# A decoder block with a product-key expert layer: the first gather tile's second half turned into a fifth dense tile

## The chip, the cores and the metric

One core of one Trainium2 chip. The metric is the device time of one execution in microseconds (us); a time of the kernel is the median of several runs. A profile is one execution more, with its own time. The engines are TensorE (PE; its weight loads are PEld), VectorE (DVE), ScalarE (ACT), GpSimd (POOL) and SyncE (SP). Each runs its instructions in the order in which they are written, and waits for the others through semaphores. SP and GpSimd issue the DMA transfers here.

## The reference

1024 tokens of width 1024 pass a mixing layer (two causal convolutions between an input and an output projection, with norms) and then the expert layer, which is nearly all of the time:

```python
q = (xf @ w_q).reshape(n_tok, PEER_HEADS, PEER_D_KEY)         # 8 heads
s1 = jnp.einsum("thd,hnd->thn", q[..., :128], sub_keys[:, 0])  # 128 keys
s2 = jnp.einsum("thd,hnd->thn", q[..., 128:], sub_keys[:, 1])
v1, i1 = lax.top_k(s1, 16)
v2, i2 = lax.top_k(s2, 16)
vals, pos = lax.top_k((v1[..., :, None] + v2[..., None, :]).reshape(..., 256), 16)
idx = e1 * 128 + e2            # e1, e2: i1, i2 at pos; 16384 experts
gates = jax.nn.softmax(vals, axis=-1)
u_sel = jnp.take(u, idx, axis=0)       # u, v: 16384 x 1024 float32, 64 MB each
act = jax.nn.gelu(jnp.einsum("chkd,cd->chk", u_sel, xc))
v_sel = jnp.take(v, idx, axis=0)
out = jnp.einsum("chk,chkd->cd", act * gates, v_sel)
```

So each token takes 8 x 16 = 128 rows of u and 128 rows of v, weighted by a gelu and a gate. The result is added to the token's row and normalised.

## The kernel before

The 1024 tokens are 8 tiles of 128. Tiles 0 to 3 (`NG`) are gather tiles: their rows of u and v are fetched one per token by indirect DMA (`fetch`, 128 x 1024 floats, 512 KB a step), 128 steps of u and 128 of v for each tile. In a u step VectorE multiplies the rows with the token's row and sums (L719); after the 128th the weights `w` are gelu times gate. In a v step VectorE adds w times the rows to the sum `prow` (L756). For tile 0 every second v step is done by ScalarE (scale, L761) and GpSimd (add to `h2`, L762).

Tiles 4 to 7 (`ND` = 4) are dense tiles: all 16384 experts are computed for their 512 tokens, and the gates decide. u and v are walked in 128 chunks of 128 experts, chunk c being all experts with first key c. For a chunk, `prep_u` transposes the rows of u on TensorE in two halves, ScalarE casts the high half `uhi`, a product with minus the identity (`minus`, L864) subtracts it, and ScalarE casts what is left as `ulo`. `hidden` multiplies in three passes (high by high, high by low, low by high: `mm3`, lines 213 to 215), 12 products of 128 x 512 for each half of the chunk. Then p = gelu, times the gates (GpSimd, L947), split into `phi` (ScalarE) and `plo` (GpSimd). Rows of v are split into `vhi` (ScalarE, L181) and `vlo` (GpSimd, L182), four buffers of each. After each group of four chunks (`GRP`), `down` multiplies the four p with the four v for all dense tiles: 8 outputs of 12 products, each added to `acc` by VectorE (L917). The rows of u and v share three buffers, `raw`.

Stages, in order: the front (projections, convolutions, norms) for tokens 0 to 511; keys, the queries of the gather half and the routing of tile 0; the front for tokens 512 to 1023 (`front(1)`), in which the gather steps begin; the routing of the dense tiles (`queries`); the gate stage (`gate_matrix`); the dense stage (`dense`). In the gate stage the experts and gates of a dense tile become one-hot rows, 8 tokens at a time (o2 and o1; of the 8 tokens of o1, `X` are done by ScalarE from a narrow one-hot `ob`, the others by VectorE, L823), and one product per token (L828) makes its 128 x 128 matrix of gates, which SP writes to memory (`gd`, L841), 32 tokens at a time, in runs of `QUAD` key chunks x 32 tokens x 4 bytes. Beside it `hidden_ahead` already computes p before the gates for the chunks in `AHEAD` (24) and stores them (`pd`, by one buffer `pa`); the dense stage loads those and computes the other 104.

The gather steps are a generator (`steps`) that the other code pulls: `advance(n)` adds n to a debt and takes a step for each whole one. The constants `PROJ`, `OUT`, `QUERY`, `GATE`, `AHD`, `HIDE`, `PACE` are what each piece of other work pulls: so they set how many gathers are issued in each stage. A gather's use comes five steps (`LAG`) behind its issue; nine buffers hold the rows. While a tile gathers, the routing of the next is done in small steps (`route_later`, every `EVERY`-th step). The order on each engine is settled when the program is built, by priorities; `mark` and `after` tie a gather's use behind the last marked instruction of its engine.

## Time and profile before

| | |
|---|---|
| median of 3 runs | 3099.85 us (3089.3 to 3113.24) |
| the profiled execution | 3104.55 us, span on the core 3102.8 us |
| TensorE, matmuls busy | 2499.2 us (81%) |
| VectorE busy | 2222.1 us (72%) |
| GpSimd busy | 1974.8 us (64%) |
| ScalarE busy | 1138.9 us (37%) |
| DMA | 838.28 MB, mean 270 GB/s |
| mean granted clock of TensorE | 0.904 |

Busy time is the share in which an engine has an instruction in hand; register, branch and semaphore instructions don't count. Matmuls overlap, and a matmul's duration includes the time in which the next has begun; the distance from start to start is what one costs in a row. "A <- B" in a wait means that the instruction A stood still until B had ended. [...] DMA share is the mean busy share of the core's 16 DMA engines.

### The profile page before, as it was taken

The page shows a single profiled execution, that of the slowest core. Times are in us where ns is not written, and L with a number is a line of the kernel's source. Part 1 is how long each engine was busy: PE and PEld are TensorE (multiplying, and loading weights), DVE is VectorE, ACT ScalarE, POOL GpSimd, SP SyncE. Part 2 cuts the span into 40 slices and gives each one's busy share as a digit, 9 for nine tenths or more (in the row PEclk, how much of TensorE's full clock was granted, in tenths as well). Part 3 has the DMA queues.
Part 4 walks back from the last instruction along what each step waited for, and adds up shares of the span by engine and source line. Part 5 has one row for each costly group of instructions (what it writes and reads, how often), then busy time and mean ns, then how long its engine had stood idle before and what let it go on. Part 6 is the DMA issues. An engine that isn't in the chain of part 4 may idle for free.

```text
span 3102.8 us, 36426 instructions
## 1 busy us (share of the span) xinstructions
PE 2499.2 (81%) x12256; PEld 2035.8 (66%) x12256; DVE 2222.1 (72%) x4518; ACT 1138.9 (37%) x1951; POOL 1974.8 (64%) x1569
## 2 busy tenths in 40 slices
PE   7988887135774688987989989899999898988993
PEld 6877675135553567775767767677777776767772
DVE  6975499899999988894565756565657565657566
ACT  3234322215433786773323233323232333232321
POOL 0002377948988533345878777778777778787774
PEclk9988999566887799998999999999999999999997
DMA  3234389776766578998989888898888888988886
GB/s 105 79 105 159 103 283 344 211 292 218 219 205 229 184 241 285 319 326 299 334 308 331 321 294 317 300 335 319 329 314 322 307 322 316 326 323 325 310 303 245
DMA packets 366571, 838.28 MB, mean 270 GB/s; under 512 B 25849, under 2 KB 184569, under 8 KB 362288
## 3 DMA queue, kind: packets, MB, share of 16 engines
q0 software_dynamic: 147456, 536.94, 48.4%
q1 hardware_dynamic: 218304, 296.85, 28.5%
q8 instruction: 96, 1.57, 0.2%
q10 hardware_dynamic: 624, 2.18, 0.2%
q14 instruction: 91, 0.75, 0.1%
HBM read 782.38 MB, written 53.48 MB: 269 GB/s over the span
## 4 chain that ended last, share of the span: by engine, by line
PE 25%; POOL 14%; issue 11%; DVE 5%; ACT 4%; DMA 4%; SPq 1%; POOLq 0%; another core or an unknown queue 0%; DVEq 0%; ACTq 0%
PE ms L215 7%; POOL g L694 7%; PE ms L214 7%; PE ms L213 7%; POOL vlo L182 4%; POOL p L947 2%; PE mm L828 2%; DVE g L719 2%; DMA raw<-in_peer_v_dram 1%; DVE prow L756 1%; PE tr L864 1%; PE tr L858 1%; ACT o L821 1%; POOL plo L182 1%; DMA g<-in_peer_u_dram,ix 1%
## 5 line engine op out<-in xcount | busy, mean ns | idle before, releaser
L694 POOL DMA_INDIRECT g<-in_peer_u_dram,ix x512 | 504.4, 985 | 389.7 <-DVE g L719 158.2
L719 DVE SCALAR_TENSOR_TENSOR g<-g,prow 128x1024 f32<-128x1024 f32 x512 | 607.5, 1216 | 119.4 <-DMA g<-in_peer_u_dram,ix 117.1
L694 POOL DMA_INDIRECT g<-in_peer_v_dram,ix x512 | 500.1, 977 | 235.1 <-DVE prow L756 120.8
L756 DVE SCALAR_TENSOR_TENSOR prow<-g,w,prow 128x1024 f32<-128x1024 f32 x450 | 578.3, 1285 | 52.7 <-DMA g<-in_peer_v_dram,ix 44.6
L917 DVE TENSOR_TENSOR acc<-acc,ms 128x512 f32<-128x512 f32 x256 | 175.6, 686 | 472.9 <-PE ms L215 409.3
L215 PE MATMUL ms<-nhi,ulo 128*128 128x512 f32 x1024 | 430.8, 421 | 33.0 <-ACT ulo L865 31.4
L213 PE MATMUL ms<-nhi,uhi 128*128 128x512 f32 x1024 | 441.6, 431 | 3.1 <-ACT pa L887 3.1
L214 PE MATMUL ms<-nlo,uhi 128*128 128x512 f32 x1024 | 424.4, 414 | 0.0
L213 PE MATMUL ms<-vhi,phi 128*128 128x512 f32 x1024 | 402.1, 393 | 1.2 <-ACT phi L181 1.2
L215 PE MATMUL ms<-vhi,plo 128*128 128x512 f32 x1024 | 399.3, 390 | 1.2 <-POOL plo L182 1.2
L214 PE MATMUL ms<-vlo,phi 128*128 128x512 f32 x1024 | 399.2, 390 | 0.0
L182 POOL TENSOR_TENSOR wlo<-wraw,whi 128x1024 fp32r<-128x1024 f32 x60 | 144.0, 2400 | 356.6 <-ACT whi L181 355.6
L182 POOL TENSOR_TENSOR vlo<-raw,vhi 128x1024 fp32r<-128x1024 f32 x128 | 307.1, 2404 | 40.1 <-ACT vhi L181 38.9
L181 ACT CAST vhi<-raw 128x1024 fp32r<-128x1024 f32 x128 | 131.2, 1049 | 505.0 <-PE ms L215 352.4
L215 PEld LDWEIGHTS ms<-nhi,ulo 128*128 128x128 f32 x1024 | 203.3, 199 | 91.4 <-ACT ulo L865 42.8
L864 PE MATMUL tr<-uhi,minus 128*128 128x512 f32 x256 | 123.7, 485 | 139.8 <-ACT uhi L862 132.8
L213 PEld LDWEIGHTS ms<-nhi,uhi 128*128 128x128 f32 x1024 | 205.4, 201 | 37.7 <-ACT pa L887 3.4
L214 PEld LDWEIGHTS ms<-nlo,uhi 128*128 128x128 f32 x1024 | 205.2, 200 | 33.1
L215 PEld LDWEIGHTS ms<-vhi,plo 128*128 128x128 f32 x1024 | 192.4, 188 | 42.5 <-POOL plo L182 2.0
L213 PEld LDWEIGHTS ms<-vhi,phi 128*128 128x128 f32 x1024 | 192.7, 188 | 40.9 <-ACT phi L181 1.6
L214 PEld LDWEIGHTS ms<-vlo,phi 128*128 128x128 f32 x1024 | 192.8, 188 | 38.1
L862 ACT CAST uhi<-tr 128x512 fp32r<-128x512 f32 x256 | 149.3, 586 | 143.4 <-PE tr L858 121.1
(213 smaller groups left out, 5110.3 us busy)
## 6 DMA issues: line engine op xcount, KB each, us to landing
raw<-in_peer_u_dram SPq DMA_DIRECT2D x128, 512.0 KB
raw<-in_peer_v_dram SPq DMA_DIRECT2D x128, 512.0 KB
gd<-st SPq DMA_DIRECT2D x64, 512.0 KB
g<-gd SPq DMA_DIRECT2D x32, 1024.0 KB
wraw<-in_w_in_dram SPq DMA_DIRECT2D x40, 512.0 KB
wraw<-in_peer_w_q_dram SPq DMA_DIRECT2D x32, 512.0 KB
wraw<-in_w_out_dram SPq DMA_DIRECT2D x16, 512.0 KB
g<-in_peer_u_dram,ix POOLq DMA_INDIRECT x512
```

The costliest lines, as they stand in the source:

```text
L181: nc.scalar.copy(hi, src)
L182: self.mark(eng.tensor_tensor(lo, src, hi.bitcast(F32), op=OP.subtract))
L213: self.nc.tensor.matmul(ps, lh(a), rh(b), start=first and i == 0, stop=False)
L214: self.nc.tensor.matmul(ps, lh(a), rl(b), start=False, stop=False)
L215: last = self.nc.tensor.matmul(ps, ll(a), rh(b), start=False, stop=final and i == n - 1)
L694: self.nc.gpsimd.indirect_dma_start(out=g, out_offset=None, in_=self.t[table][0], in_offset=bass.IndirectOffsetOnAxis(ap=ix, axis=0))
L719: self.after(nc.vector.scalar_tensor_tensor(ut, ut, 1.0, b["x"], op0=OP.mult, op1=OP.mult, accum_out=b["act"][:, k:k + 1]))
L756: self.after(nc.vector.scalar_tensor_tensor(b["h"], g, w, b["h"], op0=OP.mult, op1=OP.add))
L828: nc.tensor.matmul(pg[:, :, m], o2[:, 4 * z + m, :], o1[:, 4 * z + m, :], start=True, stop=True)
L862: self.nc.scalar.copy(hi, ps)
L864: self.nc.tensor.matmul(flat(ps), self.minus, flat(hi), start=False, stop=True, skip_group_check=True)
L917: self.mark(V.tensor_tensor(acc[:, i, dd], acc[:, i, dd], po, op=OP.add))
```

## The change

Tile 0 gathers rows of u only. Its weights `w` (`self.w0`) are kept, and in the gate stage it stands as a fifth dense tile: the same one-hot products spread its weights, instead of gates, over the experts. In the dense stage its 128 columns of p are those weights as they are (copied by ScalarE from the gates' tile `g`, no gelu and no product with u), and `down` has five tiles: 10 outputs. `NH` is now the number of tiles that are routed densely (4), `ND` the number in `down` (5). So 128 gathers of v and the `h2` sum go away.

Beside this: `AHEAD` has 40 chunks instead of 24, so 88 are computed in the dense stage. `QUAD` is 2, so a run in `gd` is 256 bytes and not 512. `X` is 4, not 6. The subtraction and the cast of the low half are a step of their own, `low_u`, tied behind the last product of the half before, and a half's transposes and `uhi` are made two halves ahead. `plo`, and `vlo` of every even chunk, move from GpSimd to VectorE. The constants of the pace are new, and tile 1 is routed in every 4th step of tile 0 (`SOON`).

```diff
 NG = NT // 2
-ND = NT - NG
+NH = NT - NG
+ND = NH + 1
 HN = NG * P
 GRP = 4
-QUAD = 4
+QUAD = 2
-AHEAD = [c for c in range(NK) if c % 16 in (5, 10, 15)]
-RATE = 0.75
+AHEAD = [c for c in range(NK) if c % 16 in (3, 6, 9, 12, 15)]
+RATE = 1.0
-AHD = 0.5
-PACE = (1, 1, 1, 2, 1, 1, 1, 2)
-HIDE = 0.85
-PROJ, OUT, QUERY, GATE = 6, 1.5, 4, 1.5
+AHD = 1
+PACE = (1,) * 10
+HIDE = 1
+PROJ, OUT, QUERY, GATE = 3, 1, 1.5, 0.8
-EVERY = 8
+EVERY, SOON = 7, 4
...
-            for part in (self.gather_up, self.gather_down):
+            for part in (self.gather_up, self.gather_down) if ti else (self.gather_up,):
...
-                    if n % EVERY == 0 and (ti == 0 or n >= LATE):
+                    if n % (EVERY if ti else SOON) == 0 and (ti == 0 or n >= LATE):
...
+                    if ti == 0:
+                        self.w0 = w
...
-        W, X, B = 8, 6, GB_T
+        W, X, B = 8, 4, GB_T
...
-                if n < len(routes):
+                if n < NH - 1:
                     nxt = self.experts(routes[n])
+                elif n == NH - 1:
+                    nxt = self.experts(self.first, self.w0)
...
         uT = [self.tile(self.de, [P, 4, P], F32R, "u" + s, bufs=3) for s in ("hi", "lo")]
+        self.nc.scalar.copy(uT[0], ps)
+        return ps, uT
+
+    def low_u(self, ps, uT):
+
         hi, lo = uT
-        self.nc.scalar.copy(hi, ps)
         flat = lambda x: x.rearrange("p a b -> p (a b)")
-        self.nc.tensor.matmul(flat(ps), self.minus, flat(hi), start=False, stop=True, skip_group_check=True)
+        self.after(self.nc.tensor.matmul(flat(ps), self.minus, flat(hi), start=False, stop=True,
+                                         skip_group_check=True))
         self.nc.scalar.copy(lo, ps)
...
                     for q in range(2):
-                        for s, ps in zip(segs, pu):
-                            self.hidden(ps, uT[q], q, s)
-                            advance(HIDE)
-                            if q == 1:
-                                nc.scalar.activation(p[:, s], ps, AF.Gelu_apprx_tanh)
+                        self.hidden(ps, made.pop(0), q, slice(0, HN))
+                        advance(HIDE)
+                        if made:
+                            made[0] = self.low_u(*made[0])
                         if main:
-                            uT[q] = self.prep_u(main[0], q)
+                            made.append(self.prep_u(*main.pop(0)))
                         advance(HIDE)
+                    nc.scalar.activation(p[:, :HN], ps, AF.Gelu_apprx_tanh)
                 pv = p.rearrange("p (b t) -> p b t", t=GB_T)
-                nc.gpsimd.tensor_tensor(pv, pv, g, op=OP.mult)
-                self.split(ph, pl, p, eng=nc.gpsimd)
+                n = HN // GB_T
+                nc.scalar.copy(pv[:, n:], g[:, n:])
+                nc.gpsimd.tensor_tensor(pv[:, :n], pv[:, :n], g[:, :n], op=OP.mult)
+                self.split(ph, pl, p)
...
-                self.split(vh, vl, self.rows_of("peer_v", c), eng=nc.gpsimd)
+                self.split(vh, vl, self.rows_of("peer_v", c), eng=nc.gpsimd if c % 2 else None)
```

**TensorE, between two halves of a chunk in the dense stage.** `ms` is the output of `hidden`, `nhi` and `nlo` the tokens, `tr` the transposed half of u. Before, the transposes of the next half stand between two halves, and its subtraction 6 products later:

```order
L213 MATMUL ms_18841<-nhi_120,uhi_18665 128x512
L214 MATMUL ms_18841<-nlo_121,uhi_18665 128x512
L215 MATMUL ms_18841<-nhi_120,ulo_18666 128x512
L858 MATMUL tr_18885<-ident_78,raw_18857 128x128 x4
L213 MATMUL ms_18910<-nhi_120,uhi_18864 128x512
L214 MATMUL ms_18910<-nlo_121,uhi_18864 128x512
L215 MATMUL ms_18910<-nhi_120,ulo_18865 128x512
L213 MATMUL ms_18910<-nhi_120,uhi_18864 128x512
L214 MATMUL ms_18910<-nlo_121,uhi_18864 128x512
L215 MATMUL ms_18910<-nhi_120,ulo_18865 128x512
L864 MATMUL tr_18885<-uhi_18890,minus_85 128x512
L213 MATMUL ms_18910<-nhi_120,uhi_18864 128x512
```

Now:

```order
L214 MATMUL ms_19471<-nhi_120,uhi_19217 128x512
L215 MATMUL ms_19471<-nlo_121,uhi_19217 128x512
L216 MATMUL ms_19471<-nhi_120,ulo_19218 128x512
L866 MATMUL tr_19246<-uhi_19251,minus_85 128x512
L856 MATMUL tr_19499<-ident_78,raw_19497 128x128 x4
L214 MATMUL ms_19471<-nhi_120,uhi_19251 128x512
L215 MATMUL ms_19471<-nlo_121,uhi_19251 128x512
L216 MATMUL ms_19471<-nhi_120,ulo_19252 128x512
L214 MATMUL ms_19471<-nhi_120,uhi_19251 128x512
L215 MATMUL ms_19471<-nlo_121,uhi_19251 128x512
L216 MATMUL ms_19471<-nhi_120,ulo_19252 128x512
```

The subtraction stands at the end of a half and is that of the half which follows at once (`uhi_19251`); the transposes behind it belong to the half after that. The third product of the half is the first to read `ulo_19252`.

**GpSimd before, at the end of a `down`.** `vlo` and `vhi` are the split v, `raw` its rows, `g` a gathered tile:

```order
L694 DMA g_18854<-in_peer_v_dram,ix_14601 128x1024
L182 TENSOR_TENSOR vlo_18833<-raw_18834,vhi_18832 128x1024
L694 DMA g_18881<-in_peer_v_dram,ix_14601 128x1024
L182 TENSOR_TENSOR vlo_18902<-raw_18903,vhi_18901 128x1024
L694 DMA g_18895<-in_peer_v_dram,ix_14601 128x1024
L694 DMA g_18923<-in_peer_v_dram,ix_14601 128x1024
L694 DMA g_18938<-in_peer_v_dram,ix_14601 128x1024
L694 DMA g_18953<-in_peer_v_dram,ix_14601 128x1024
L947 TENSOR_TENSOR p_18840<-p_18840,g_18608 128x512
L694 DMA g_18978<-in_peer_v_dram,ix_14601 128x1024
L182 TENSOR_TENSOR plo_18839<-p_18840,phi_18838 128x512
L182 TENSOR_TENSOR vlo_18985<-raw_18986,vhi_18984 128x1024
```

**VectorE now, at the same place.** `prow` lines are gather steps of v, `acc` the last outputs of a `down`:

```order
L918 TENSOR_TENSOR acc_11718<-acc_11718,ms_19409 128x512
L759 SCALAR_TENSOR_TENSOR prow_18149<-g_19327,w_18122,prow_18149 128x1024
L183 TENSOR_TENSOR plo_19450<-p_19451,phi_19449 128x640
L183 TENSOR_TENSOR vlo_19444<-raw_19445,vhi_19443 128x1024
L918 TENSOR_TENSOR acc_11718<-acc_11718,ms_19426 128x512
L759 SCALAR_TENSOR_TENSOR prow_18149<-g_19344,w_18122,prow_18149 128x1024
L759 SCALAR_TENSOR_TENSOR prow_18149<-g_19372,w_18122,prow_18149 128x1024
L759 SCALAR_TENSOR_TENSOR prow_18149<-g_19389,w_18122,prow_18149 128x1024
L183 TENSOR_TENSOR vlo_19544<-raw_19545,vhi_19543 128x1024
L759 SCALAR_TENSOR_TENSOR prow_18149<-g_19406,w_18122,prow_18149 128x1024
L759 SCALAR_TENSOR_TENSOR prow_18149<-g_19423,w_18122,prow_18149 128x1024
L183 TENSOR_TENSOR plo_19469<-p_19470,phi_19468 128x640
```

The `plo` and the `vlo` of even chunks stand among VectorE's gather steps; the `vlo` of odd chunks have stayed on GpSimd.

**SP in the gate stage, before.** `st` is 32 tokens' gates, four transfers each:

```order
L888 DMA pd_112<-pa_9343 128x512
L841 DMA gd_113<-st_9162 128x8x128 x4
L849 DMA raw_9816<-in_peer_u_dram 128x1024
L502 DMA sck_17304<-sd_114 128x256
L888 DMA pd_112<-pa_9559 128x512
L849 DMA raw_9958<-in_peer_u_dram 128x1024
L841 DMA gd_113<-st_9436 128x8x128 x4
L888 DMA pd_112<-pa_9704 128x512
L849 DMA raw_10103<-in_peer_u_dram 128x1024
```

Now:

```order
L847 DMA raw_9187<-in_peer_u_dram 128x1024
L847 DMA raw_9293<-in_peer_u_dram 128x1024
L847 DMA raw_9401<-in_peer_u_dram 128x1024
L894 DMA pd_112<-pa_9062 128x512
L839 DMA gd_113<-st_8855 128x16x64 x4
L894 DMA pd_112<-pa_9247 128x512
L847 DMA raw_9507<-in_peer_u_dram 128x1024
L894 DMA pd_112<-pa_9350 128x512
L847 DMA raw_9615<-in_peer_u_dram 128x1024
L839 DMA gd_113<-st_9143 128x16x64 x4
L894 DMA pd_112<-pa_9461 128x512
```

A transfer has 16 runs of 64 floats for each partition where it had 8 of 128; a store of early p now stands right ahead of each group of four and right behind it or the next load.

## Rows read from the trace of the kernel before

**Rows 1.** Stages: us, then PE, PEld, DVE, ACT, POOL busy, clock, DMA share, GB/s

```profile
397.00:795.00 398.00, 213.58 (x964) 173.38 (x963) 362.94 (x699) 115.28 (x150) 308.84 (x243) 0.74 0.79 273
795.00:1008.00 213.00, 144.04 (x643) 113.36 (x643) 206.81 (x964) 80.47 (x102) 182.03 (x116) 0.81 0.68 218
1008.00:1400.00 392.00, 326.29 (x1959) 276.67 (x1959) 344.76 (x834) 302.30 (x676) 152.73 (x116) 0.92 0.84 272
1400.00:3068.00 1668.00, 1489.69 (x6597) 1180.15 (x6595) 1019.84 (x1321) 501.21 (x795) 1282.48 (x1065) 0.95 0.87 315
```

**Rows 2.** Timeline of TensorE: start us, us, engine, line, operation, tiles

```profile
1117.05 1.05 PE L828 MATMUL mm<-o,o 128*128 128x128 f32 x8
1117.86 0.48 PE L864 MATMUL tr<-uhi,minus 128*128 128x512 f32 x1
...
2005.78 0.60 PE L858 MATMUL tr<-ident,raw 128*128 128x128 f32 x4
...
2012.78 0.60 PE L858 MATMUL tr<-ident,raw 128*128 128x128 f32 x4
...
2020.60 0.39 PE L213 MATMUL ms<-vhi,phi 128*128 128x512 f32 x1
...
2037.61 0.39 PE L213 MATMUL ms<-vhi,phi 128*128 128x512 f32 x1
```

**Rows 3.** Waits of the dense stage (1400 to 3068): total us, times, longest

```profile
ACT phi L181 <- POOL p L947: 186.6, 96, 8.3
...
PE tr L864 <- ACT uhi L862: 121.3, 58, 8.2
...
ACT vhi L181 <- DMA raw<-in_peer_v_dram: 152.6, 48, 9.2
...
PE ms L215 <- ACT ulo L865: 26.9, 13, 9.7
```

**Rows 4.** Timeline of one stall at a group's start, four engines

```profile
1980.16 2.00 ACT L181 CAST vhi<-raw 128x1024 fp32r<-128x1024 f32 x2 [15.43 <-PE ms L215]
...
1986.26 2.42 POOL L182 TENSOR_TENSOR vlo<-raw,vhi 128x1024 fp32r<-128x1024 f32 x1
...
1988.70 0.85 SPq L849 DMA_DIRECT2D raw<-in_peer_v_dram  x2
...
1996.44 1.04 ACT L181 CAST vhi<-raw 128x1024 fp32r<-128x1024 f32 x1 [9.24 <-DMA raw<-in_peer_v_dram]
...
1998.51 0.79 PE L864 MATMUL tr<-uhi,minus 128*128 128x512 f32 x1 [8.24 <-ACT uhi L862]
```

**Rows 5.** VectorE groups, 397 to 795, last row 795 to 1008: busy, mean ns

```profile
L719 DVE SCALAR_TENSOR_TENSOR g<-g,prow 128x1024 f32<-128x1024 f32 x128 | 153.1, 1215 | 21.8 <-DMA g<-in_peer_u_dram,ix 21.3
...
L756 DVE SCALAR_TENSOR_TENSOR prow<-g,w,prow 128x1024 f32<-128x1024 f32 x18 | 22.9, 1273 | 0.0
...
L756 DVE SCALAR_TENSOR_TENSOR prow<-g,w,prow 128x1024 f32<-128x1024 f32 x30 | 38.1, 1270 | 3.1 <-DMA g<-in_peer_v_dram,ix 3.1
```

**Rows 6.** Groups of the whole run, shapes apart: busy us, mean ns, idle before

```profile
L182 POOL TENSOR_TENSOR vlo<-raw,vhi 128x1024 fp32r<-128x1024 f32 x128 | 307.1, 2404 | 40.1 <-ACT vhi L181 38.9
...
L917 DVE TENSOR_TENSOR acc<-acc,ms 128x512 f32<-128x512 f32 x256 | 175.6, 686 | 472.9 <-PE ms L215 409.3 <-PE ms L214 25.4 <-issue 19.2
...
L814 DVE TENSOR_TENSOR o<-iota,eT 128x1024 f32<-128x1024 f32 x64 | 81.3, 1270 | 27.8 <-PE mm L828 22.0 <-remote 4.0 <-PE tr L858 1.5
...
L823 DVE TENSOR_SCALAR o<-iota,eT 128x128 f32<-128x128 f32 x128 | 40.9, 375 | 0.0
...
L182 DVE TENSOR_TENSOR wlo<-wraw,whi 128x1024 fp32r<-128x1024 f32 x28 | 34.2, 1223 | 18.7 <-ACT whi L181 18.4
```

**Rows 7.** DMA queue 1, gate stage then dense: packets, MB, share of 16 engines

```profile
q1 hardware_dynamic: 71584, 52.47, 42.5%
...
q1 hardware_dynamic: 45952, 167.37, 28.3%
```

**Rows 8.** Line 841 (gates to memory): duration ns min/median/max, first and last start

```profile
L841 SPq DMA_DIRECT2D gd<-st x64: 370/1192/10117, 1054.6 to 1393.5; - x64
```

More of the change, by code (lines that the diff above doesn't have):

```diff
@@ L483, in queries_gather @@
         w_q = self.t["peer_w_q"][0].rearrange("(k p) n -> p k n", p=P)
-        tiles = val, ind, best, slot = self.route_tiles(self.lz)
+        tiles = self.first = val, ind, best, slot = self.route_tiles(self.lz, kept=self.keep)
         with self.pool("scan", 2) as scan:
@@ L604, in lists, with experts @@
         return lst
-    def experts(self, r):
+    def experts(self, r, weights=None):
         V = self.nc.vector
@@ L741, in gather_down @@
         b = {}
-        side = range(1, HK - 4, 2) if ti == 0 else ()
         def step(k):
@@ L901, in dense @@
         self.banks(3, 0, 3)
+        rows = [NG + i for i in range(NH)] + [0]
         with self.pool("dn", 2, right=True) as dn:
             acc = self.tile(dn, [P, ND, D], F32, "acc", bufs=1)
-            for i in range(ND):
-                nc.sync.dma_start(acc[:, i, :], self.h_d[(NG + i) * P:(NG + i + 1) * P])
-            segs = segments(T)
+            for i, r in enumerate(rows):
+                nc.sync.dma_start(acc[:, i, :], self.h_d[r * P:(r + 1) * P])
             pend = []
@@ L919, in down @@
                     if final:
-                        self.finish(NG + i, acc[:, i, :])
-            main = [c for c in range(NK) if c not in AHEAD]
-            uT = [self.prep_u(main[0], q) for q in range(2)]
+                        self.finish(rows[i], acc[:, i, :])
+            main = [(c, q) for c in range(NK) if c not in AHEAD for q in range(2)]
+            made = [self.low_u(*self.prep_u(*main.pop(0))), self.prep_u(*main.pop(0))]
             for c in range(NK):
```

73 lines of the change are left out of this document (32 added, 41 removed).

## The prediction

> **What bounds the kernel now.** I read the stages first [rows 1]: columns are length, then busy time of TensorE's matmuls, its weight loads, VectorE, ScalarE and GpSimd, the granted clock, the DMA share and rate. Four stretches matter. In the second front (397 to 795) and the dense routing (795 to 1008) VectorE is busy 362.94 of 398 and 206.81 of 213 us: VectorE sets both. In the gate stage (1008 to 1400) VectorE has 344.76, TensorE 326.29 and ScalarE 302.30 of 392: three engines take turns. In the dense stage (1400 to 3068) TensorE has 1489.69 of 1668, GpSimd 1282.48 and VectorE only 1019.84; the DMA share is 0.87.
>
> Busy time hides a part of what TensorE loses, so I take the pitch instead [rows 2]. From the first transposes of one chunk to those of the next are 2012.78 - 2005.78 = 7.00 us (24 products, 8 transposes, 2 subtractions). In the `down` part 75 products lie between 2020.60 and 2037.61: 0.2268 us each. In the gate stage eight one-hot products take 1117.86 - 1117.05 = 0.81 us, 0.101 each. Dense needs 104 x 7.00 + 3072 x 0.2268 = 728 + 697 = 1425 us without a stall; it takes 1668, so 243 are lost: 178 idle, the rest slow pitches (granted clock 0.95). The gate stage needs 24 x 7.00 + 1024 x 0.101 + some 8 for the small transposes = 280 of 392: 112 lost.
>
> Then the waits of the dense stage [rows 3]: 121.3 of the 178 idle us are the subtraction (`minus`, L864) waiting for its high half `uhi`, 26.9 more are products waiting for `ulo`. ScalarE works in order, so the question is what it stands at instead: 152.6 us for the raw rows of v and 186.6 us for `p` from GpSimd. One such stall in full [rows 4]: `down` has ended, `vhi` is cast twice from 1980.16, GpSimd makes the two `vlo`, the second from 1986.26 for 2.42 us, only then does SP issue the next v load (1988.70, its `raw` slot has come free), the next `vhi` starts at 1996.44, and TensorE's subtraction, whose `uhi` stood behind it, starts at 1998.51 after 8.24 us idle.
>
> **The change part by part.** *Second front.* The order lists give 168 gathers issued on GpSimd by its end before, 96 now. VectorE ran 128 u products (153.1 us, so 1.196 each) and 18 v products (22.9) there [rows 5]. Now it has about 91 (96 less the lag of 5): 91 x 1.196 = 109, so 67 us less; as VectorE holds 91% of the stage, and fewer gathers are waited for, I take -75. Bounds: -45 if the chain from TensorE through the normalisations takes over, -95 if all idle of VectorE goes too. Tile 1's routing keeps its number of steps (every 8th of 168, now every 4th of 96).
>
> *Dense routing.* 30 v products (38.1 us [rows 5]) go; 23 u products (27) come: -11. GpSimd no longer adds the `h2` rows, which ran beside VectorE. I take -15, bounds 0 and -30.
>
> *Gate stage.* TensorE: 40 x 7.00 + 1280 x 0.101 + 10 = 419 us, +139. VectorE: the wide one-hots o2 81.3 x 80/64 = +20; the narrow ones go from 2 to 4 of 8 tokens, 128 to 320 at 40.9/128 = 0.320: +61 [rows 6]; a fifth `experts`, some +10; gathers in the stage 106 to 73 by the lists, about -33 u products or -39. So VectorE has about 345 + 52 = 397. TensorE becomes the longest of the three. The floor is 419 plus the start (TensorE waits for the first routing); with all of the old loss it is 531. The high halves now stand a half chunk ahead, and ScalarE loses a share of the one-hots, so I take 482, nearer the middle: +90. Bounds +50 and +139.
>
> *Dense.* 16 chunks leave and a fifth tile comes to every `down`: 88 x 7.00 + 3840 x 0.2268 = 616 + 871 = 1487, +62 of work that nothing hides. Against it stands the loss of 243. Three edits work on it. First, the subtraction now stands behind the last product of the half before, on a high half cast a half chunk earlier, so the 121.3 us lose their direct cause; what can wait in its place is the third product of a half, for `ulo`. That cast has the 4 transposes and two products to hide in, about 0.36 + 2 x 0.23 us behind the subtraction, against one cast of 0.59: just covered, as long as ScalarE is free. If it stands at `vhi`, TensorE still stops after 24 + 2 products, hardly later than before (24 + 6). Second, therefore, the raw loads: half of the `vlo` go to VectorE, 1.223 us (`wlo`, same shape [rows 6]) instead of 2.404 on GpSimd. In the stall of [rows 4] the two `vlo` would lie side by side, and the load would go out some 4 to 6 us earlier; most of that stall goes. Third, GpSimd loses 64 x 2.404 = 154 us and all `plo`, so `p` comes sooner. I let the loss fall from 243 to 125: dense 1612, -56. It is the choice with the widest bounds: at 50 it is 1537 (-131), at the old 243 it is 1730 (+62).
>
> VectorE pays in dense: 64 additions to `acc` at 0.686 (44), 64 `vlo` (78), 128 `plo` of 640 columns (from 1.223 for 1024, about 0.8: 102), 23 more gathers (28): 1020 + 252 = 1272 of 1612, 79%. It has room on the mean. Behind a product that waits for its gather stand now a `plo` and a `vlo`; TensorE needs the `plo` of a group only when the next chunk's 7 us are through, which is the cover; without it each such wait is TensorE's. ScalarE's additions (128 more columns per `phi`, a small copy) hide in its 70% idle. DMA moves, by the lists, 541 MB instead of 525: 336 GB/s for 315, which brings the share to about 0.93.
>
> *End.* 13 v products were left behind the last addition, now 7: 6 x 1.27 = -8.
>
> **Sum.** -75 - 15 + 90 - 56 - 8 = -64, on the profiled execution's 3104.55: 3040 us. That run lies 4.7 us above the median of 3099.85, which I neglect.
>
> **The write of the gates** has a price that no row shows. Two key chunks instead of four stand together in `gd`, so runs are 256 bytes, not 512, and 64 transfers become 80 with 163,840 runs instead of 65,536. In the gate stage queue 1 holds 42.5% of 16 engines, 2666 engine-us, for 52.47 MB, of which 33.55 are these runs; its other 18.9 MB at dense's 45.1 engine-us per MB (28.3% for 167.37 MB) are 853 [rows 7], so a run costs 27.7 ns. All other transfers of the new gate stage (40 loads of u, 73 gathers, 40 stores of p, some 3 MB more: 73 MB at 45.1) come to 206 us of 16 engines. If a short run costs half, `gd` takes 142 and the sum is 348: hidden in 482. If it costs as much as a long one, 284 and 490: about the stage itself. If it costs two long ones, 567 and 773. I take a price between the first two, which goes with most of the old run being bytes (a 4 KB packet of the same queue takes 185 ns, so 27.7 for 512 is almost in proportion). SP is also held longer: 1.192 us in the median for one transfer of 1024 runs [rows 8], so about 2.4 x 80 = 191 us of the stage, and the u loads and the stores of the early `p` (one buffer) queue behind it; u loads are two chunks, over 20 us, ahead.
>
> [...]
>
> **Rivals.** *A, slower: VectorE takes GpSimd's place.* `plo` and `vlo` stand behind gather products in VectorE's order, the raw loads and the `down` parts start as late as before, and the losses stay at 243 and 112. Then -75 - 15 + 139 + 62 - 8 = +103: 3207. For it: VectorE at 79% in order; DMA share 0.93. Against it: [rows 4], where the second `vlo` on GpSimd is the link. It decides from the point where the two losses, 355 together, fall by less than 201 - 98 = 103.
> *B, slower: short runs at double price.* The gate stage is set by DMA at 773 instead of 482: 3040 + 291 = 3331.
> *C, no change.* The losses fall by about a third only, TensorE eats what the fronts save: about 3100. The added 201 us of products are certain, the relief is not.
>
> **Chances.** Forecast 0.56 with its own range 2960 to 3068; C 0.18; A 0.18; B 0.08. One per cent is about what a measurement of this kernel can tell from no change, so faster (under 3069) 0.56, same 0.18, slower 0.26. The low end comes from the good ends of dense (-100), fronts (-110) and gate (+70): 2960. The high end reaches to A, 3205, and leaves out B and a strip below: about 2 in 10.
>
> **What would show it.** Right: no waits of the subtraction for `uhi` worth naming, TensorE idle in dense near 100 us, the gate stage at some 480 us with TensorE over 85% busy, the second front near 323. Wrong: VectorE waits ahead of `plo` that TensorE waits for (A); a DMA share at 1 in the gate stage with ScalarE or TensorE waiting for `raw`, `pd` or `st` (B); `ulo` in place of `uhi` with the same sum (A or C). The forecast falls if gate and dense together take over 2158 us.

## The result: 3071.3 us, ratio 0.991, where 3040 was forecast

The changed kernel takes 3071.3 us (median of 9 runs, 3062.5 to 3077.5) against 3099.85 before (also 9 runs): ratio 0.9907, interval 0.9884 to 0.9929, a gain of 28.6 us. Forecast was a gain of 60. The time lies inside the range, at the edge between the forecast and the rival "no change", but the sum was wrong by half of its gain. The profiled execution took 3074.73 us (before 3104.55).

Stages of the changed kernel (us, then busy time of PE, PEld, DVE, ACT, POOL, the granted clock of TensorE as a share of full speed, DMA share, GB/s), the stretches that answer to [rows 1]:

```profile
397.00:692.00 295.00, 208.08 (x966) 171.53 (x965) 261.82 (x583) 89.60 (x126) 199.00 (x155) 0.80 0.70 235
692.00:870.00 178.00, 134.21 (x633) 107.52 (x634) 177.54 (x1033) 46.80 (x71) 56.81 (x38) 0.86 0.42 131
870.00:1327.00 457.00, 436.89 (x2792) 384.04 (x2791) 363.12 (x1054) 316.21 (x719) 78.75 (x71) 0.98 0.88 242
1327.00:3040.00 1713.00, 1563.73 (x6828) 1244.41 (x6828) 1279.96 (x1581) 488.91 (x840) 1042.47 (x900) 0.96 0.88 318
```

| stage | before | forecast | after | off by |
|---|---|---|---|---|
| second front | 398 | 323 | 295 | -28 |
| dense routing | 213 | 198 | 178 | -20 |
| gate stage | 392 | 482 | 457 | -25 |
| dense stage | 1668 | 1612 | 1713 | +101 |
| end | 35 | 27 | 33 | +6 |

Four terms had the right sign, and three of them came out 20 to 28 us better than forecast. The dense stage, the term with the widest bounds, went the other way: of its 1487 us of work without a stall (616 + 871, as in the prediction) it takes 1713, a loss of 226 where 243 were lost before and 125 were forecast.

Waits of its dense stage (total us, times, longest), answering to [rows 3]:

```profile
DVE plo L183 <- ACT phi L182: 193.1, 78, 8.1
ACT ulo L868 <- PE tr L866: 152.0, 65, 5.9
...
ACT phi L182 <- POOL p L949: 109.5, 92, 3.2
ACT vhi L182 <- DMA raw<-in_peer_v_dram: 89.4, 49, 5.1
PE tr L856 <- DMA raw<-in_peer_u_dram: 76.6, 27, 8.5
PE ms L216 <- ACT ulo L868: 42.6, 31, 2.2
```

The 121.3 us of the subtraction waiting for `uhi` are gone, as forecast, and ScalarE waits less for `p` and for v. In their place TensorE's transposes wait 76.6 us for raw rows of u, which the kernel before hardly did (the same view of its dense stage):

```profile
PE tr L858 <- DMA raw<-in_peer_u_dram: 9.7, 6, 2.8
```

The wait for `ulo`, on the third product, where the prediction had looked for it, is 42.6 us, 26.9 before. Idle time of TensorE in the dense stage: 1713 - 1564 = 149 us, before 178. So 77 us of the loss (226 - 149) are products at a slower pace, before 65 (243 - 178).

The costliest groups that answer to [rows 5] (VectorE, 397 to 692) and to [rows 6] (whole run, shapes apart):

```profile
L723 DVE SCALAR_TENSOR_TENSOR g<-g,prow 128x1024 f32<-128x1024 f32 x87 | 103.8, 1210 | 11.3 <-DMA g<-in_peer_u_dram,ix 11.1
```

```profile
L918 DVE TENSOR_TENSOR acc<-acc,ms 128x512 f32<-128x512 f32 x320 | 219.1, 685 | 191.3 <-PE ms L216 177.2 <-issue 13.2 <-remote 0.6
...
L183 POOL TENSOR_TENSOR vlo<-raw,vhi 128x1024 fp32r<-128x1024 f32 x64 | 154.6, 2416 | 25.4 <-ACT vhi L182 23.1 <-PE tr L856 1.5
...
L183 DVE TENSOR_TENSOR plo<-p,phi 128x640 fp32r<-128x640 f32 x128 | 133.8, 1045 | 193.3 <-ACT phi L182 193.1
...
L183 DVE TENSOR_TENSOR vlo<-raw,vhi 128x1024 fp32r<-128x1024 f32 x64 | 78.3, 1223 | 50.1 <-ACT vhi L182 44.0 <-issue 6.1
```

`vlo` on VectorE costs what the row of `wlo` said (1223 ns); `plo` costs 1045 where 0.8 us was estimated.

### The profile page after: what moved, and what is told of

The parts are those of the page before. It is cut to its first block, busy times and chain, and to the rows that moved or that the text cites. A ratio compares the mean times of both kernels' runs of the same rounds, so it can differ in the third digit from the quotient of the medians.

```text
span 3073.0 us, 38845 instructions
## 1 busy us (share of the span) xinstructions
PE 2669.3 (87%) x13313; PEld 2200.9 (72%) x13313; DVE 2363.6 (77%) x4947; ACT 1082.5 (35%) x1985; POOL 1420.8 (46%) x1188
## 4 chain that ended last, share of the span: by engine, by line
PE 36%; DVE 21%; issue 15%; DMA 12%; POOL 12%; ACT 3%; SPq 1%; POOLq 0%; DVEq 0%; ACTq 0%
PE ms L216 8%; PE ms L214 8%; PE ms L215 8%; POOL g L698 7%; DMA raw<-in_peer_u_dram 5%; DVE g L723 4%; PE mm L826 4%; DMA raw<-in_peer_v_dram 2%; DVE prow L759 2%; DVE tr L302 2%; POOL p L949 2%; PE mm L214 2%; POOL vlo L183 2%; PE mm L215 2%; DMA p<-pd 2%
## 5 line engine op out<-in xcount | busy, mean ns | idle before, releaser
L214 PE MATMUL ms<-vhi,phi 128*128 128x512 f32 x1280 | 509.4, 398 | 20.4 <-ACT phi L182 19.7
L698 POOL DMA_INDIRECT g<-in_peer_v_dram,ix x384 | 385.3, 1003 | 283.4 <-DVE prow L759 200.8
L216 PE MATMUL ms<-vhi,plo 128*128 128x512 f32 x1280 | 505.1, 396 | 5.9 <-DVE plo L183 5.9
L215 PE MATMUL ms<-vlo,phi 128*128 128x512 f32 x1280 | 506.0, 395 | 1.1 <-POOL vlo L183 1.1
L759 DVE SCALAR_TENSOR_TENSOR prow<-g,w,prow 128x1024 f32<-128x1024 f32 x384 | 493.2, 1284 | 5.1
L214 PEld LDWEIGHTS ms<-vhi,phi 128*128 128x128 f32 x1280 | 244.7, 191 | 75.4 <-ACT phi L182 24.0
L183 DVE TENSOR_TENSOR plo<-p,phi 128x640 fp32r<-128x640 f32 x128 | 133.8, 1045 | 193.3 <-ACT phi L182 193.1
L215 PEld LDWEIGHTS ms<-vlo,phi 128*128 128x128 f32 x1280 | 244.8, 191 | 51.8 <-POOL vlo L183 1.4
L856 PE MATMUL tr<-ident,raw 128*128 128x128 f32 x1024 | 195.8, 279 | 77.2 <-DMA raw<-in_peer_u_dram 76.6
L949 POOL TENSOR_TENSOR p<-p,g 128x512 f32<-128x512 f32 x128 | 175.3, 1370 | 102.1 <-ACT p L945 61.2
```

Of the source, the lines that this page charges most:

```text
L183: self.mark(eng.tensor_tensor(lo, src, hi.bitcast(F32), op=OP.subtract))
L214: self.nc.tensor.matmul(ps, lh(a), rh(b), start=first and i == 0, stop=False)
L215: self.nc.tensor.matmul(ps, lh(a), rl(b), start=False, stop=False)
L216: last = self.nc.tensor.matmul(ps, ll(a), rh(b), start=False, stop=final and i == n - 1)
L698: self.nc.gpsimd.indirect_dma_start(out=g, out_offset=None, in_=self.t[table][0], in_offset=bass.IndirectOffsetOnAxis(ap=ix, axis=0))
L759: self.after(nc.vector.scalar_tensor_tensor(b["h"], b.pop(k), res[0][:, k:k + 1], b["h"], op0=OP.mult, op1=OP.add))
```

## One stall of the new kind

Timeline of the changed kernel (a second profiled execution, that of "The changed kernel again" below, span 3057.7 us): start us, us, engine, operation, and in brackets the idle time before it and what ended it.

```profile
1924.41 1.23 DVE L183 TENSOR_TENSOR vlo<-raw,vhi 128x1024 fp32r<-128x1024 f32 x1 [1.61 <-ACT vhi L182]
...
1925.02 1.77 POOL L949 TENSOR_TENSOR p<-p,g 128x512 f32<-128x512 f32 x1 [1.59 <-ACT p L945]
...
1926.82 0.33 SPq L928 DMA_DIRECT2D g<-gd  x1
1927.25 0.37 SPq L847 DMA_DIRECT2D raw<-in_peer_u_dram  x1
...
1931.57 0.60 PE L856 MATMUL tr<-ident,raw 128*128 128x128 f32 x4
...
1934.34 0.37 SPq L847 DMA_DIRECT2D raw<-in_peer_u_dram  x1
...
1937.39 0.44 PE L856 MATMUL tr<-ident,raw 128*128 128x128 f32 x1 [4.75 <-DMA raw<-in_peer_u_dram]
```

The transposes at 1937.39 wait for the u load issued at 1927.25, 10.1 us before; the DMA share is 0.93 ahead of the idle time and 1.00 behind it (the stretches below). A raw buffer had been free since VectorE's `vlo` ended at 1925.64. But on SP the u load stood behind the load of the gates (`g`), which waited for GpSimd's `p` until 1926.79. The u load at 1934.34 is the one after it.

Most waits are of this kind. In the profiled execution of the result, 22 of the 27 waits for raw rows (65.4 of the 76.6 us) are for a u load that stands directly behind a load of gates on SP, in the kernel before none. `QUAD` = 2 makes 64 such loads of 32, and SP stands longer at them in the dense stage, first before, then now:

```profile
SPq L927 <- POOL p L947: 80.8, 29, 5.9
```

```profile
SPq L928 <- POOL p L949: 246.5, 60, 17.3
```

No run takes this part of the change back by itself, so its share of the loss stays open.

TensorE also asks for the rows earlier. By the program the transposes stand where they stood: in both lists of TensorE's order they follow the last product of a half and belong to the half after the next. What was moved is the subtraction, from 4 to 7 products behind its transposes to 12. But the order that the builder makes now takes some transposes ahead (profiled execution of the result):

```profile
2093.31 0.60 PE L856 MATMUL tr<-ident,raw 128*128 128x128 f32 x4
...
2094.22 0.27 PE L856 MATMUL tr<-ident,raw 128*128 128x128 f32 x1
...
2097.17 0.49 PE L856 MATMUL tr<-ident,raw 128*128 128x128 f32 x3
```

Two products lie between the first two of these rows, where the kernel before has twelve ([rows 2] shows its four at once). That is ten products earlier, about 2.3 us at [rows 2]'s 0.2268 each. It happens at 62 halves of the dense stage, in the kernel before at none, and 54.7 of the 76.6 us are waits there.

The stall costs more than its length. The same execution in stretches (columns as above), before the stall, right behind it, and after that:

```profile
1925.00:1932.60 7.60, 7.19 (x33) 5.39 (x33) 5.66 (x9) 4.96 (x10) 5.79 (x5) 1.00 0.93 308
1937.40:1943.00 5.60, 5.60 (x16) 4.43 (x17) 0.47 (x1) 0.73 (x2) 3.19 (x3) 0.51 1.00 377
1943.00:1948.00 5.00, 5.00 (x25) 4.03 (x25) 4.19 (x8) 3.03 (x7) 1.93 (x2) 1.00 0.93 334
```

For 5.60 us behind the idle time the granted clock is 0.51, and 16 matmuls run where the next 5.00 us hold 25: some 2.7 us more are lost (5.60 x 0.49). Two more stalls of this execution end in the same way (0.58 for 5.40 us behind a wait of 4.67, 0.65 for 4.60 us behind one of 4.18). In the first experiment below, with 57 waits for `uhi` of at most 3.1 us each, the dense stage's clock is 0.99.

## The experiments

In each expectation the theories are those of that run. Chips differ: the kernel before took 3069.9 us on one (the second four runs) and 3096 to 3106 on the others, so times are compared within a group, and between groups only as ratios to the kernel before.

### The parts of the change, one at a time

**The low half at once again**, in the changed kernel:

```diff
         self.nc.scalar.copy(uT[0], ps)
...
+        self.nc.tensor.matmul(flat(ps), self.minus, flat(uT[0]), ...)
+        self.nc.scalar.copy(uT[1], ps)
         return ps, uT
     def low_u(self, ps, uT):
-        (subtraction and cast)
         return uT
```

> The changed kernel, but the subtraction and the cast of the low half are made at once with the transposes again, as before. Theory 1 (the raw buffers): TensorE's lost time in the dense stage (1713 us for 1487 of products) is set by when the rows of u and v arrive in their three buffers, and the moved low half has only changed the place where TensorE stands and waits: waits of the subtraction for uhi come back, those of the transposes for raw u (76.6 us) shrink by about as much, time 3060 to 3090. Theory 2 (the order): the move took away most of the 121 us of waits and other edits brought new ones: dense stage 1790 to 1830, time 3150 to 3190.

Measured 3009.4 us, ratio 0.9715 (0.9687 to 0.9742). That is 54 to 60 us less than the changed kernel by the ratios (0.9889 and 0.9907 in two measurements). Neither theory had it. The dense stage takes 1640, with TensorE busy 1518.59 and idle 121. Its waits:

```profile
PE tr L861 <- ACT uhi L859: 81.2, 57, 3.1
...
PE tr L856 <- DMA raw<-in_peer_u_dram: 29.8, 12, 11.7
```

The transposes stand twelve products or more apart again, closer at two halves only. So the edit that the prediction called the first of three reliefs was a loss. Of the 73 us between the two dense stages 28 are idle time and 45 are slower products (1564 to 1519 busy, clock 0.96 to 0.99).

**The splits back on GpSimd**, all `plo` and all `vlo`:

```diff
-                self.split(ph, pl, p)
+                self.split(ph, pl, p, eng=nc.gpsimd)
...
-                self.split(vh, vl, ..., eng=nc.gpsimd if c % 2 else None)
+                self.split(vh, vl, ..., eng=nc.gpsimd)
```

> The changed kernel, but plo and all vlo on GpSimd as before. Theory 1 (the raw buffers): a slow vlo holds a raw buffer 1.2 to 4 us longer in each of 32 groups, and p and plo queue with it on GpSimd: dense stage 1760 to 1840, time 3110 to 3200. Theory A of the prediction (VectorE's order is itself in the way): dense stage 1650 to 1700, time 3010 to 3060.

3120.2 us, ratio 1.006 (1.004 to 1.008): some 50 us more than the changed kernel, inside the first theory's band of time. Its mechanism is not borne out: TensorE's wait for raw rows does not grow (69.4 us for 76.6), the one for `ulo` does (67.0 for 42.6). VectorE does not take GpSimd's place; it relieves it (rival A falls).

**The moved low halves alone**, put into the kernel before (`low_u` and the loops over half chunks, nothing else):

> The kernel before with one part of the change alone: the low halves moved behind the half before, high halves made two ahead. Theory 1 (the raw buffers): the waits move from the subtraction to the transposes and to ulo, sum of TensorE's idle in the dense stage still 140 to 180 us, time 3075 to 3110. Theory 2 (the order): the 121.3 us of waits for uhi go and half of the slow clock behind them, time 2970 to 3030.

3097.6 us, ratio 1.000 (0.998 to 1.002). Waits of its dense stage (1386 to 3058.5):

```profile
PE ms L215 <- ACT ulo L870: 120.5, 48, 8.1
...
PE tr L858 <- DMA raw<-in_peer_u_dram: 42.5, 25, 5.3
```

The 121.3 us for `uhi` have become 120.5 for `ulo` (26.9 before) and 42.5 for raw rows (9.7 before). The wait moved, and nothing was gained: the first theory.

**A fourth raw buffer**, in the changed kernel (a gather buffer is given up for it):

```diff
-GB, LAG = 9, 5
+GB, LAG = 8, 5
...
-            ... F32, "raw", bufs=3)
+            ... F32, "raw", bufs=4)
```

> The changed kernel with four raw buffers for the rows of u and v instead of three, and, to make room, eight gather buffers instead of nine. Theory 1 (the raw buffers): waits of the transposes for raw u fall from 76.6 to under 25 us, dense stage 1620 to 1670, time 2980 to 3030. Rival (DMA: the loads arrive late because 318 GB/s are in flight, whatever buffer is free): waits of the transposes and of vhi stay within 20%, time 3060 to 3090 (the gather buffer may cost some 10).

2996.1 us, ratio 0.9663 (0.9635 to 0.9691), dense stage 1629. The wait for raw rows of u falls from 76.6 to 3.7 us, though the DMA moves 334 GB/s in that stage for 318: the first theory, and its rival falls.

### A control, both cures together, the tie, and GpSimd's load

**Eight gather buffers, three raw buffers** (the control of the run above):

> The changed kernel with eight buffers for gathered rows instead of nine, nothing else: the control of the run with four raw buffers, which gave up the same ninth buffer. Theory 1 (the time lay in the fourth raw buffer): 3071 to 3085 us, TensorE's waits for raw rows of u in the dense stage stay at 65 to 90 us. Theory 2 (fewer gathers in flight relieve the DMA engines, and that gave the gain): 2995 to 3030 us with the waits for raw u under 30 us.

3054.7 us, ratio 0.9969 (0.9942 to 0.9996) on the chip where the kernel before takes 3069.9; raw rows of u are waited for 68.6 us. The time is below the 3071 to 3085 of the first theory and far above the second's. The chip is another, so the waits decide, and they are the first theory's: the gain was the raw buffer's (the square below shows it on one chip).

**Both cures**, low half at once and four raw buffers:

> The changed kernel with the low half subtracted and cast at once again AND four raw buffers (eight gather buffers). Alone the first gave 3009 us and the second 2996, from 3071. Theory 1 (two different losses: ScalarE standing at ulo, and loads that go out late because three raw buffers are full; what was left in the first run, 81 us of waits for uhi behind a late vhi, is the second loss and goes too): 2930 to 2970 us, dense stage about 1590 us, waits for uhi under 40 us. Theory 2 (both removed the same idle time, and what is left is the pace of the products at this clock): 2980 to 3000 us, dense 1625 or more.

3021.3 us, ratio 0.9848 (0.9802 to 0.9893): outside both bands, above the second theory's. So the two cures do not add. As the chip was another one, the square below repeats it.

**The subtraction without its tie** (`self.after(...)` taken off, the builder's priorities place it):

> The changed kernel with the low half still a step of its own and the high half still a half chunk ahead, but the subtraction no longer tied behind the last marked product: the builder's priorities place it. Theory 1 (what costs is the high half cast far ahead and the cast of the low half standing in ScalarE's order in front of vhi and phi, wherever the tie puts the subtraction by one or two places): 3055 to 3080 us, TensorE still waits 30 us or more for ulo. Theory 2 (the tie itself costs, it holds the subtraction back): 3005 to 3030 us with the waits for ulo under 15 us.

3056.8 us, ratio 0.9962 (0.993 to 0.9995), waits for `ulo` 38.2 us. That is the first theory: the wait for raw rows is 61.2 us, and the builder takes the transposes ahead at 62 halves here too. So the tie is not what costs. The changed kernel with nine gather buffers was not run on this chip; with eight it took 3054.7 there.

**64 useless additions on GpSimd**, beside the u steps of tile 0:

```diff
+                if ti == 0 and k % 2:
...
+                    nc.gpsimd.tensor_tensor(self.h2, self.h2, ut, op=OP.add)
```

> The changed kernel with eight gather buffers, and on GpSimd an addition of the gathered 128x1024 rows to a tile that nobody reads, after every second u step of the first gather tile (64 additions of about 2.4 us, nearly all in the second front). It adds work of no use on GpSimd alone; VectorE's instructions are the same. Theory 1 (VectorE's own instructions take longer while GpSimd computes; that is why the second front and the dense routing shrank by 28 and 20 us more than the removed products): VectorE busy in the second front 20 to 50 us above that of the control with eight buffers, for the same instructions, and the stage 20 to 50 us longer; whole time 20 to 60 us above it. Theory 2 (the shorter time came from fewer gathers in flight or a shorter chain): VectorE's busy time for the same instructions unchanged to within 5 us, the stage longer only if something waits for GpSimd.

3131.3 us, 76.6 above the control (the kernel with eight gather buffers, same chip). From 397 us to the first one-hot product of the gate stage (control, then this run):

```profile
397.00:877.40 480.40, 332.10 (x1584) 270.81 (x1583) 440.13 (x1612) 139.37 (x198) 253.32 (x192) 0.84 0.58 192
```

```profile
397.00:948.20 551.20, 350.70 (x1598) 280.87 (x1597) 515.50 (x1684) 138.59 (x199) 390.26 (x249) 0.79 0.53 168
```

GpSimd is busy 137 us more and VectorE 75, with the same 111 u products and 72 small instructions more. That is the first theory, with more than its 20 to 50 us. What grows are single instructions, first in the control and then here:

```profile
L322 DVE SCALAR_TENSOR_TENSOR sc<-z,cols,sc 128x512 f32<-128x512 f32 x8 | 10.4, 1299 | 0.0
```

```profile
L322 DVE SCALAR_TENSOR_TENSOR sc<-z,cols,sc 128x512 f32<-128x512 f32 x8 | 29.4, 3675 | 0.0
```

One of them in the timeline of this run:

```profile
676.33 1.42 POOL L698 DMA_INDIRECT g<-in_peer_u_dram,ix  x1 [0.30 <-DVE g L723]
...
677.26 5.47 DVE L161 TENSOR_SCALAR lna<-lna 128x512 f32<-128x512 f32 x1
...
677.77 2.37 POOL L729 TENSOR_TENSOR h<-h,g 128x1024 f32<-128x1024 f32 x1
...
680.09 2.34 POOL L183 TENSOR_TENSOR wlo<-wraw,whi 128x1024 fp32r<-128x1024 f32 x1
```

In the control this instruction takes 415 ns. Here it stands in VectorE for 5.47 us. GpSimd is busy without a break from 676.33, and the instruction ends at 682.73, just behind GpSimd's last at 682.43: it stood until the third of three GpSimd instructions in a row had ended. By what it was held is not shown. The u products, whose second operand is in PSUM (`to_psum`), take 1208 ns in the control and 1210 here.

### The square: raw buffers by low half, on one chip

All four with eight gather buffers; corner 2 is corner 1 with the edit of the first experiment, corner 3 with the fourth raw buffer, corner 4 with both.

> Corner 1 of a square of four on one chip, all with eight gather buffers, because the runs of one raw buffer more and of both edits were made on two chips on which the kernel before took 3100.7 and 3069.9 us. This corner: the changed kernel, three raw buffers, low half a half chunk later. Theory 1 (the two edits remove different losses) and theory 2 (the fourth raw buffer cures what made the moved low half costly, so that the low half at once is no gain any more with four buffers) expect the same here: the slowest corner, about 0.985 to 0.997 of the kernel before.

> Corner 2: three raw buffers, the low half subtracted and cast at once. Both theories: 30 to 65 us below corner 1, dense stage 1620 to 1650 us.

> Corner 3: four raw buffers, the low half moved. Both theories: 40 to 75 us below corner 1, TensorE's waits for raw rows of u under 10 us.

> Corner 4: four raw buffers and the low half at once. Theory 1: below corners 2 and 3 both, by 20 us or more. Theory 2: 10 to 30 us above corner 3, since TensorE then waits some 80 us in the dense stage for uhi at the subtraction, where corner 3 waits some 50 us for ulo.

| | low half moved | low half at once |
|---|---|---|
| three raw buffers | 3057.3 us, dense 1692 | 3021.8 us, dense 1657 |
| four raw buffers | 2993.0 us, dense 1632 | 3025.0 us, dense 1656 |

Ratios to the kernel before: 0.9872, 0.977, 0.9662, 0.9775, each within 0.003. With three raw buffers the moved low half costs 36 us; with four it gains 32. And a fourth buffer gives 64 us to the moved low half and nothing to the other. That is the second theory (corner 4 lies 32 us above corner 3, 2 us beyond its band). TensorE's wait of corner 3 and that of corner 4 say why the sign turns:

```profile
PE ms L216 <- ACT ulo L868: 51.1, 40, 2.6
```

```profile
PE tr L861 <- ACT uhi L859: 83.9, 51, 4.9
```

With four buffers the waits for raw rows are small (3.4 us in corner 3, 14.0 in corner 4), and these two waits differ by 33 us, the dense stages by 24. With three the dense stages of corners 1 and 2 read:

```profile
1333.00:3025.00 1692.00, 1549.33 (x6828) 1236.02 (x6828) 1296.19 (x1581) 488.51 (x840) 1043.87 (x901) 0.97 0.89 322
```

```profile
1331.00:2988.00 1657.00, 1523.92 (x6828) 1213.44 (x6828) 1293.52 (x1582) 495.54 (x840) 1048.14 (x901) 0.98 0.90 329
```

Idle time is 143 and 133 us, so 25 of the 35 us are slower products. Where the rows come late, the move trades many short waits for `uhi` against fewer and longer ones for the rows: in corner 2 TensorE waits 63 times for `uhi` (89.8 us, at most 3.9) and 12 times for raw rows of u (24.8 us), in corner 1 25 times for raw rows (71.4 us, at most 8.7). That the builder's early transposes make this, and not the later subtraction, is not shown: no run keeps them at their place with the cast moved.

### What was left open: before, the splits apart, the short runs

**The changed kernel again**, to read the next two against:

> The changed kernel itself, on the same chip as the next three, since the kernel before took 3069.9 to 3100.7 us on the chips so far. Either theory: 0.987 to 0.997 of the kernel before; it is what the next two are read against.

3067.7 us, ratio 0.9889 (0.9864 to 0.9914).

**`vlo` alone back on GpSimd**, then **`plo` alone** (the two lines of the diff above, one each):

> The changed kernel with every vlo on GpSimd again; plo stays on VectorE. With both on GpSimd it took 49 us more. Theory 1 (vlo holds the raw buffer of v, so that its time is what the next load and the next transposes wait for; plo frees no raw buffer): 30 to 55 us above the changed kernel, TensorE's waits for raw rows of u in the dense stage 100 us or more. Theory 2 (plo is what TensorE waited for, or GpSimd's load as a whole): 0 to 20 us above it.

3141.4 us, ratio 1.0121 (1.0089 to 1.0152): 74 us more than the changed kernel, above the first theory's band. TensorE waits 61.1 us for raw rows, where that theory had 100 or more, and 97.4 for `ulo`. ScalarE, which makes `ulo`, waits longer for the rows of v, first in the changed kernel again, then here:

```profile
ACT vhi L182 <- DMA raw<-in_peer_v_dram: 86.8, 45, 6.6
```

```profile
PE ms L216 <- ACT ulo L868: 97.4, 35, 6.2
...
ACT vhi L182 <- DMA raw<-in_peer_v_dram: 119.1, 39, 7.4
```

So a later `vlo` does delay the next rows, but those of v, and by them probably `ulo`.

> The changed kernel with plo alone on GpSimd again; half of the vlo stay on VectorE. Theory 1 (the splits act apart: vlo back +74, both back about +50, so plo back alone -20): 0.980 to 0.986 of the kernel before, some 10 to 30 us below the changed kernel, with VectorE's waits for phi (some 190 us in the dense stage) gone and a smaller wait of TensorE for ulo. Theory 2 (GpSimd's order is the link: each plo there stands in front of a vlo, so it matters only with all vlo there): 0.987 to 1.000 of the kernel before, no faster than the changed kernel.

3071.0 us, ratio 0.9912 (0.9883 to 0.9942): no change. The second theory. With four raw buffers:

> The changed kernel with four raw buffers (eight gather buffers) and plo on GpSimd again. With four raw buffers alone it took 0.966 of the kernel before. Theory 1: 0.955 to 0.962, since VectorE's gather steps no longer stand behind a plo that waits for phi. Theory 2: 0.966 to 0.980, since GpSimd's plo delays its vlo and p.

3057.6 us, ratio 0.9861 (0.9823 to 0.99), where VectorE's `plo` gave 0.966: the move of `plo` is worth 62 us there, more than either theory had. TensorE's wait for `ulo` is 98.2 us, and the clock 0.96 instead of 0.99. By these runs `plo` on VectorE gains only once the raw rows come in time. Why `vlo` alone back costs more than `vlo` and `plo` together stays open.

**Long runs written, short runs read.** The changed kernel writes 256-byte runs and reads them back in whole rows; here it writes 512-byte runs and reads 256-byte pieces (the layout of `gd` with blocks of four chunks):

> The changed kernel with the gates' matrix written in runs of 512 bytes again (blocks of four key chunks) and still read by two chunks, so in runs of 256 bytes: only the write in the gate stage differs. Theory 1 (the gate stage is bound by TensorE, busy 437 of 457 us, and the short runs hide behind it, though they hold the queue 54 us longer): within 10 us of the changed kernel, gate stage 450 to 460 us, queue 1 in that stage with under 50% of 16 engines instead of 62%. Theory 2 (the short runs delay the loads and stores of the early p and so the stage): 15 to 40 us faster, gate stage 420 to 440 us.

3090.0 us, ratio 0.9954 (0.9936 to 0.9971), 22 us slower: outside both bands. The gate stage takes 455 us, as in the changed kernel on this chip. Queue 1 in it (packets, MB, share of 16 engines), first in the changed kernel, answering to [rows 7], then here:

```profile
q1 hardware_dynamic: 177377, 73.48, 62.3%
```

```profile
q1 hardware_dynamic: 94646, 73.91, 52.4%
```

So the short runs are hidden in the gate stage, as the first theory has it (its "under 50%" was a little low). The 22 us lie in the dense stage (1700 to 1722), where 204420 packets replace some 47,700 and copies wait 55.6 us for `g`: the expectation had overlooked that reading changes too. What a written run of 256 bytes costs follows from the changed kernel's gate stage, by the method of the prediction (an estimate): 62.3% of 16 x 457 us are 4555 engine-us; less 1422 for the other 31.5 MB, by 163,840 runs, that is 19.1 ns against 27.7 for 512 bytes.

**The kernel before with a fourth raw buffer:**

> The kernel before with four raw buffers and eight gather buffers, nothing else. Theory 1 (the raw buffers became the bound through the change, which transposes a half chunk earlier; before, TensorE waited for uhi behind ScalarE, in order, and a fourth buffer does not shorten GpSimd's vlo): 3085 to 3110 us, waits for uhi still 90 us or more in the dense stage. Theory 2 (the late loads were the root of the loss before too): 3020 to 3060 us, waits for uhi under 60 us.

3079.7 us, ratio 0.9923 (0.9895 to 0.995), 5 us below the first theory's band. The dense stage takes 1663 us (1668 in [rows 1]), and TensorE waits 136.8 us for `uhi` (121.3 in [rows 3]): the first theory, for that stage. Of the profiled execution's 23 us, 18 lie ahead of it (the first one-hot of the gate stage starts at 1019 instead of 1036 us). A gather buffer less is the only other edit, and no run of the kernel before has that alone.

## Why the prediction was right or wrong, step by step

**The step that failed** is the first of the three that were to bring the dense loss from 243 to 125: "the subtraction now stands behind the last product of the half before, on a high half cast a half chunk earlier, so the 121.3 us lose their direct cause". They did lose it. But in the dense stage the high half is not cast earlier by the program; the subtraction comes later. I then asked only whether the cast of `ulo` was covered, and not what the new order does to the link ahead of it: the builder takes the transposes ahead, so the raw rows must be there earlier, with the same three buffers, and on SP their loads stand behind twice as many loads of gates. TensorE's wait for raw rows of u went from 9.7 to 76.6 us, in single waits of up to 8.5, and the clock fell behind the long ones (0.51 for 5.60 us behind one of 4.75). The square puts a number on it: +36 us with three buffers, -32 with four. With the fourth buffer the dense stage takes 1629 to 1632 us, near the 1612 forecast for the change as it stood.

**The second step**, that `vlo` on VectorE lets the loads go earlier, was right: taken back alone it costs 74 us, and ScalarE waits 119.1 us for rows of v instead of 86.8. **The third**, that GpSimd without `plo` brings `p` sooner, has no worth in this kernel (0.9912 with `plo` on GpSimd, 0.9889 to 0.9907 with it on VectorE). So the term was a relief of some 74, less a loss of some 36 to 60 that I had booked as a relief, if the two add up, which no run shows. The 62 us of added work were right as far as can be seen: the loss of 226 is counted against them.

**The fronts** were right in kind and too small. 103.8 us of u products in place of 153.1 and 22.9 are 72 us, where 67 were forecast; but VectorE's busy time fell by 101. The rest is other and shorter instructions beside a GpSimd that is busy 199.00 us there and was 308.84. One group of the dense routing, before and after:

```profile
L554 DVE TENSOR_TENSOR cand<-val 128x16 f32<-128x16 f32 x10 | 14.3, 1428 | 0.0
```

```profile
L556 DVE TENSOR_TENSOR cand<-val 128x16 f32<-128x16 f32 x12 | 1.9, 160 | 0.0
```

The run with useless additions shows that effect and its size: 75 us of VectorE for 137 of GpSimd. My sum had priced GpSimd's dropped work at nothing, because it "ran beside VectorE".

**The gate stage** was forecast at 482, between a floor of 419 and all of the old loss. It takes 457, with TensorE busy 436.89: 96% where "over 85%" was asked. The loss fell from 112 to 38 us, nearer the floor than I chose; no run here shows why.

**The write of the gates.** The value taken, between half a long run and a whole one, was right: 19.1 ns, 0.69 of 27.7. SP's hold per transfer is about what I put (2.31 us in the median for 2.4), and hidden; the row that answers to [rows 8]:

```profile
L839 SPq DMA_DIRECT2D gd<-st x80: 370/2312/7836, 901.9 to 1321.7; - x80
```

The third case, two long runs' time for a short one (55.4 ns), is not what these rows show. B is priced with it; the estimate from the changed kernel's gate stage is 19.1 ns.

**The rivals.** A fell (both splits back on GpSimd cost 50 us). B fell (19.1 ns). C said that the losses fall by about a third only and TensorE eats what the fronts save. The losses did fall by about a quarter (355 to 264), nearly all in the gate stage; the fronts saved 138 us where 90 were forecast, and that kept C from being the result. I had named "`ulo` in place of `uhi` with the same sum" as the sign of C; the sign that came, raw rows of u, I had not named for the dense stage.

**The better version** is the change with a fourth raw buffer: 0.966 of the kernel before, in two measurements on two chips.

## What to carry to other kernels

When the order of an engine changes, follow every link behind it back to a buffer: what is now read earlier must be there earlier too, and if the ring of buffers is the same, the wait can just change its name, as the 121.3 us for `uhi` became 120.5 for `ulo` and 42.5 for raw rows. Read where the builder really puts the steps around it, and which loads stand in front on the queue. Test a cure and the resource that it needs as a pair: here one alone cost 36 us and the other alone gained nothing. And price the work taken from GpSimd by what VectorE does beside it, not at nothing: 137 us more of GpSimd stood beside 75 more of VectorE here.

## What was not expected of the hardware

- A VectorE instruction stood until three GpSimd instructions in a row had ended: 415 ns became 5.47 us beside GpSimd instructions of 1.42, 2.37 and 2.34. The u products, which take an operand from PSUM, did not change (1208 and 1210 ns).
- One idle stretch of 4.75 us of TensorE was followed by 5.60 us at a granted clock of 0.51, so this wait cost about half as much again. The 57 waits for `uhi` of at most 3.1 us each, in the first experiment, stand in a stage with a clock of 0.99.
- TensorE's transposes started 10.1 us after the issue of their 512 KB load of u rows (1927.25, the stall above), with the DMA share at 0.93 ahead of the idle time and 1.00 behind it. In the profile of the kernel before, transposes at 2519.29 that waited for such a load started 3.82 us after its issue (2515.47), at a share of 0.66.
- On one chip the kernel before took 3069.9 us, on the others 3096 to 3106, while the changed kernel with eight gather buffers took 3054.7 and 3057.3: the same edit was worth 0.3% on one chip and 1.3% on another. No run shows why.
